# Two-layer encoder trunk, one core: the last token tile's norm and the routing around it

## Chip, core and metric

The kernel runs on one core of one Trainium2 chip. The metric is the device time of one execution in microseconds (us), lower is better. The kernel before takes 1039.52 us, the median of three runs between 1038.59 and 1041.96 us.

## The reference, cut to what matters

Each of two layers mixes 512 tokens of width 1024 and then sends every token to two of sixteen small experts. The change lies between the two parts:

```
x    = _layernorm(DEEPNORM_ALPHA * x + mix, ln1_g[l], ln1_b[l])
glog = einsum('bsd,dg->bsg', x, wg) + bg         # 4 group logits
gp, gi = top_k(softmax(glog), 1)                 # best group
elog = einsum('bsd,gde->bsge', x, we) + be       # 4 expert logits in each group
ep, ei = top_k(softmax(elog of group gi), 2)     # best two experts
h    = silu(x @ w_gate[e]) * (x @ w_up[e]) * combine
out  = h @ w_down[e]
```

The kernel has no top_k. It counts ranks by comparisons, and so gets for every token and expert a place in that expert's block of 96 rows.

## The kernel before, in words

The 512 tokens are four tiles of 128 (t0 to t3). Within a layer, after the mixer, the string `WSEQ` gives the order in which the steps of the four tiles are traced; a planner at compile time then orders each engine's instructions by that order and by when it reckons their inputs to be ready. `tc.issue_after(ins)` puts what is traced in its block behind `ins` on that instruction's own engine, in order of issue only. `pin` keeps instructions behind the one traced before them on their engine.

The steps of one tile i are: `m`/`n`/`o` products with the output projection; `e` evacuation, four transposes (TensorE) and a copy (ScalarE, `cp`); `b` mean and variance; `r` the reciprocal root; `l` eight small products with the routers' weights and `c` the correction of the logits by mean and root; `g` and `f` the norm itself, `(x - mean) * gain` and `* root + bias`; `k` a store to `acc`. `f` ends with the store of the tile to `x1d` (L1804), from which the experts' rows are gathered. Of the norm's 1024 columns the first `PHS[i]` = 512 go over ScalarE and GpSimd (L1793, L1801), the rest over VectorE. `Kab` is `route(a, b)` for tiles a to b-1: `ranks` and comparisons on VectorE, down to the mark `al` (which experts a token has); a product of `al` with a strict triangle and with ones (TensorE); `key` (the place in the block); and the one-hots `ohf` and `ohs` of experts 0 and 1.

Expert 0's rows are not gathered. `Zi` (`xz`) multiplies tile i with `ohf`, sixteen products, and sums all four tiles in two PSUM banks; after Z3 they are split in a high and a low part. `H` is `ex[1].go()`: products that give the row numbers of expert 1 (`slx`), and on GpSimd's queue the indirect gather from `x1d` (L1447), which needs the stores of all four tiles. Behind it on GpSimd stands a memset (`mark`), and loads of weights traced after it wait for that (`held`).

Then come the weights of the tokens (softmax values, some thirty small VectorE instructions), and `all_experts`: 24 products with the first weights of expert 0 (`up`), transposes of expert 1's gathered rows (`x`), and then a fixed order per expert. SyncE issues the weights' loads in the planner's order, and so does it with the stores.

Of the kernel before, what the change touches and what calls it, by code (L numbers as in the profile page):

```python
# [2 lines left out]

# [6 lines left out]
F32 = mybir.dt.float32  # L10
F32R = mybir.dt.float32r
BF = mybir.dt.bfloat16
I32 = mybir.dt.int32
# [4 lines left out]
D = 1024  # L18
# [66 lines left out]
HK = 0  # L85
HE = 0
WSEQ = ('S0 S1 S2 A m0 e0 b0 r0 r0 r0 r0 g0 A m1 e1 b1 r1 r1 r1 r1 g1 l0 c0 f0 k0 A m2 l1 c1 K02 e2 b2 r2 r2 r2 r2 g2 f1 k1 '
        'A n3 l2 c2 K23 Z0 o3 e3 b3 r3 r3 g3 r3 r3 l3 c3 f2 k2 K34 Z1 Z2 f3 H Z3')
WPIN = ''
NU = 7  # L90
WOG = (0, 2)
PTV = range(8)
GSEQ = 'gzgzgzgzzz'
PHS = (512, 512, 512, 512)
SQ = (0, 1, 2, 3)
SQN = ((), (0, 1, 2, 3))
PHASE = None
# [114 lines left out]
def tile_trunk(ctx: ExitStack, tc: tile.TileContext, ins, out, dbg=None, depth=DEPTH):  # L212
# [191 lines left out]
    V.memset(t64, 0.0)  # L404


    def split(dst_h, dst_l, src, eng=V):
        r = A.activation(dst_h, src, AF.Copy)
        eng.tensor_sub(dst_l, src, dst_h.bitcast(F32))
        return r  # L410

    def pair(src=None):
# [145 lines left out]
    for l in range(depth):  # L558
# [678 lines left out]
        def mla_in():  # L1237
            for i in range(2):
                b, h, lo = pair()
                split(h[64:96], lo[64:96], kra[64:96])  # L1240
                V.tensor_copy(h[96:128], h[64:96].bitcast(F32))
                V.tensor_copy(lo[96:128], lo[64:96].bitcast(F32))
# [36 lines left out]
            mla.update(rots=rots, qn=qn, kn=kn, uk=uk[0], vt=vt)  # L1279
            router_sums()  # L1280
            yield

        def load_uq(g):
# [124 lines left out]
        class Expert:  # L1408
# [56 lines left out]
            def xz(self, i, z):  # L1465
# [1 line left out]
                if i == 0:  # L1467
                    self.px = [P4.get(4 * BLK) for _ in range(2)]
                for k in range(KD):
                    T.matmul(self.px[k // 4][:, (k % 4) * BLK:(k % 4 + 1) * BLK], z[:, k * 128:(k + 1) * 128],  # L1470
                             self.ohf[:, i], start=i == 0 and k % 4 == 0, stop=i == NT - 1, skip_group_check=True)
                if i == NT - 1:
                    self.gth, self.gtl = Q.get(1024, full=True), Q.get(1024, full=True)
                    for q in range(2):
                        w = slice(q * 4 * BLK, (q + 1) * 4 * BLK)
                        split(self.gth[:, w], self.gtl[:, w], self.px[q].ap)
                    free(self.px)

            def weights(self, wts):

# [239 lines left out]
        prk = []  # L1720

        def route(a, b):

# [8 lines left out]
            V.tensor_tensor(al[:, a:b].rearrange("p i (g e) -> p i g e", g=4), oa[:, a:b], bc(oh1[:, a:b, 0]), op=OP.mult)  # L1732
            if not prk:
                prk.append(P5.get(NT * E))
            p = prk[0]
# [8 lines left out]
                T.matmul(v[:, i + 1:b], onesb, al[:, i, None, :].to_broadcast([128, b - 1 - i, E]),  # L1744
                         start=False, stop=False, skip_group_check=True)
            if a:
                T.matmul(p[:, a * E:b * E], strict, al[:, a:b].rearrange("p i e -> p (i e)"), start=False, stop=True,
                         skip_group_check=True)
            r = V.scalar_tensor_tensor(key[:, a:b], v[:, a:b], 1.0, al[:, a:b], op0=OP.add, op1=OP.mult)
            for e in range(2):  # L1750
                ex[e].hot(key[:, :, e], a, b)
# [2 lines left out]
        class Tile_:  # L1754
# [42 lines left out]
            def f(self):  # L1797
                z, n = self.z, self.ph
                if n:
                    self.cp = A.activation(z[:, 0:n], z[:, 0:n], AF.Identity, scale=self.rs)  # L1800
                    G.tensor_add(z[:, 0:n], z[:, 0:n], ln1[1][:, 0:n])  # L1801
                if n < D:
                    V.scalar_tensor_tensor(z[:, n:], z[:, n:], self.rs, ln1[1][:, n:D], op0=OP.mult, op1=OP.add)
                self.st = nc.sync.dma_start(x1d[self.s, :], z.ap)  # L1804

            def keep(self):
# [10 lines left out]
        for c in WSEQ.split():  # L1817
            if c[0] == "Z":
                i = int(c[1])
                ex[0].xz(i, tiles[i].z)  # L1820
                if i < NT - 1:
                    tiles[i].z.free()
                continue
# [12 lines left out]
            if c[0] == "S":  # L1836
# [2 lines left out]
                pin[0] = False  # L1839
                continue  # L1840
            t = tiles[int(c[1])]
            pin[0] = WPIN
            {"m": t.mm, "n": lambda: t.mm(range(PROG, 3)), "o": lambda: t.mm((3,)), "e": t.evac, "b": t.bn, "r": t.r, "l": t.logits, "c": t.lgs, "g": t.g, "f": t.f, "k": t.keep}[c[0]]()
            pin[0] = False
# [19 lines left out]
        ahead(RES3)  # L1864


        lv = lg.rearrange("p i (g e) -> p i g e", g=5)
        m1, m2 = small([128, NT, 5], tag="m1"), small([128, NT, 4], tag="m2")
        V.tensor_reduce(m1, lv, axis=AX.X, op=OP.max)
        ge = small([128, NT, 4], tag="ge")  # L1870
        V.tensor_tensor(ge, lv[:, :, 0], bc(m1[:, :, 0]), op=OP.subtract)
        A.activation(ge, ge, AF.Exp)
        gs = small([128, NT], tag="gs")
        V.tensor_reduce(gs, ge, axis=AX.X, op=OP.add)
        el2 = small([128, NT, 4, 4], tag="el2")
        V.scalar_tensor_tensor(el2, oh1[:, :, 1:5], NEG, lv[:, :, 1:5], op0=OP.mult, op1=OP.add)
        V.tensor_reduce(m2, el2, axis=AX.X, op=OP.max)
        V.tensor_sub(m2, m2, m1[:, :, 1:5])
        V.tensor_mul(m2, m2, oh1[:, :, 0])
        md = small([128, NT], tag="md")  # L1880
        V.tensor_reduce(md, m2, axis=AX.X, op=OP.add)
        A.activation(md, md, AF.Exp)
        wgt = small([128, 2, NT], tag="wgt")
        V.scalar_tensor_tensor(wgt[:, 0], md, 1.0, gs, op0=OP.add, op1=OP.mult)
        V.tensor_scalar(wgt[:, 0], wgt[:, 0], ALPHA, None, op0=OP.mult)
        V.reciprocal(wgt[:, 0], wgt[:, 0])
        V.tensor_mul(wgt[:, 1], wgt[:, 0], md)

        wt, wu = small([128, NT, E], tag="wt"), small([128, NT, 4, 4], tag="wu")
        wv = wt.rearrange("p i (g e) -> p i g e", g=4)  # L1890
        V.tensor_tensor(wu, oa, oh1[:, :, 1:5], op=OP.subtract)
        for o, c in ((wu, 1), (wv, 0)):
            V.tensor_tensor(o, wu if c else oh1[:, :, 1:5], wgt[:, c, :, None, None].to_broadcast([128, NT, 4, 4]), op=OP.mult)
        V.tensor_add(wv, wv, wu)
        V.tensor_tensor(wv, wv, ogx, op=OP.mult)
        for c in range(3):
            V.tensor_copy(tokw[:, :, :, c], wt)
            if c < 2:
                V.tensor_sub(wt, wt, tokw[:, :, :, c])

        pcn = P5.get(E)
        for i in range(NT):
            T.matmul(pcn.ap, onesb, al[:, i], start=(i == 0), stop=(i == NT - 1))
        more = small([128, 3, E], tag="more")
        nb, inc, off = more[:, 0], more[:, 1], more[:, 2]
        V.tensor_scalar(nb, pcn.ap, float(BLK), None, op0=OP.is_gt)
        for c in range(2 * BLK, S, BLK):
            V.scalar_tensor_tensor(nb, pcn.ap, float(c), nb, op0=OP.is_gt, op1=OP.add)
        pcn.free()
        V.tensor_tensor_scan(inc, nb, nb, 0.0, op0=OP.add, op1=OP.bypass)  # L1910
        V.tensor_sub(off, inc, nb)
        nblk = small([1, 1], I32, tag="nblk")
        V.tensor_copy(nblk, inc[0:1, E - 1:E])
        tap("lg%d" % l, lg.rearrange("p i c -> p (i c)"))
        tap("key%d" % l, key.rearrange("p i c -> p (i c)"))

        ph("moe")

        def all_experts():


            fw, fr, fr2 = (None, None), None, None
            for e in range(2):
                ex[e].weights(tokw[:, :, e, :])
            for q in range(4):
                ex[0].up(q)
            if E > 1:
# [303 lines left out]
```

## Time and profile before

| | us |
|---|---|
| median of three runs | 1039.52 |
| profiled execution, its own time | 1042.05 |
| span of the profiled execution | 1040.3 |

The span is the time from the first to the last instruction; the rest of the profiled execution's time lies around it. Its mean granted TensorE clock is 0.984 of full speed. Routing of layer 0 lies at about 320 to 349 us of the span, that of layer 1 at about 832 to 861 us. A timeline row gives the start, the busy time, the engine, the line, the operation and in brackets the engine's idle time before it with what ended it; a row may stand for several instructions (x16), whose times lie within it.

### The profile page before, as it was taken

To read this page: it belongs to the slowest core of one execution; us is meant where nothing else is said; L and a number is where in the kernel's file an instruction comes from. 1 tells how busy PE (TensorE), PEld (TensorE's weight loads), DVE (VectorE), ACT (ScalarE), POOL (GpSimd) and SP (SyncE) were. 2 spreads that over 40 slices of the span, in tenths; PEclk is the share of its full clock that TensorE was granted. 3 is DMA by queue.
4 is the path that set the end of the run, shared out by engine and by line. 5 is a ranking of instruction groups with operands and counts; after the bars stand their busy time and mean duration, and the time that the engine had idled before them with its cause. 6 is when DMAs were issued, how large, how long until landed. Compare 5 with 4: busy or idle time off the path is not lost. (4 is left out here: it accounts for less than half of the span.)

```text
span 1040.3 us, 15380 instructions
## 1 busy us (share of the span) xinstructions
PE 984.0 (95%) x5326; PEld 735.5 (71%) x5326; DVE 814.4 (78%) x1808; ACT 636.2 (61%) x1176; POOL 192.4 (18%) x176
## 2 busy tenths in 40 slices
PE   6999999999998999999899999999999989999995
PEld 6976697666687666766598767885757876666663
DVE  7996556878639799999778956578795498999986
ACT  5565625576424588889546556465673246888874
POOL 1000001242003133232000000022420122333332
PEclk9999989999999899999899999999999989999998
DMA  8201100015855889998541101001358387999944
GB/s 313 71 21 65 67 1 1 25 55 185 282 184 212 286 273 342 340 328 275 190 163 57 55 31 61 1 1 41 115 166 311 138 281 260 331 340 328 317 118 161
DMA packets 51793, 176.74 MB, mean 170 GB/s; under 512 B 8169, under 2 KB 8681, under 8 KB 51712
## 3 DMA queue, kind: packets, MB, share of 16 engines
q1 hardware_dynamic: 45216, 160.42, 43.3%
q0 software_dynamic: 6496, 15.31, 6.1%
q8 instruction: 42, 0.69, 0.3%
q14 instruction: 39, 0.32, 0.1%
HBM read 159.61 MB, written 23.59 MB: 176 GB/s over the span
## 5 line engine op out<-in xcount | busy, mean ns | idle before, releaser
L229 PE MATMUL b<-xt,s 128*128 128x512 f32 (+3 forms) x1484 | 327.4, 368 | 12.5 <-ACT s L229 8.5
L229 PE MATMUL b<-s,s 128*128 128x512 f32 (+8 forms) x1312 | 323.4, 404 | 4.7 <-ACT s L229 2.9
L229 PEld LDWEIGHTS b<-xt,s 128*128 128x128 f32 (+2 forms) x1484 | 234.8, 184 | 79.4 <-issue 12.8
L229 DVE TENSOR_TENSOR s<-s,s 128x1024 fp32r<-128x1024 f32 (+8 forms) x252 | 226.5, 924 | 53.1 <-ACT s L229 45.6
L229 ACT ACTIVATE s<-s 128x1024 fp32r<-128x1024 f32 (+4 forms) x221 | 192.3, 904 | 89.7 <-PE b L229 32.6
L229 PEld LDWEIGHTS b<-s,s 128*128 128x128 f32 (+3 forms) x1312 | 183.4, 171 | 85.9 <-ACT s L229 18.6
L229 ACT ACTIVATE s<-b 128x512 f32<-128x512 f32 (+8 forms) x274 | 132.2, 500 | 179.3 <-PE b L229 174.1
L229 PE MATMUL b<-s,xt 128*128 128x256 f32 (+2 forms) x944 | 204.6, 357 | 0.3 <-DVE s L229 0.3
L229 PEld LDWEIGHTS b<-s,xt 128*128 128x128 f32 (+1 forms) x944 | 147.9, 187 | 33.9 <-issue 6.9
L229 DVE TENSOR_TENSOR xt<-s,xt 128x1024 fp32r<-128x1024 f32 (+1 forms) x106 | 125.9, 1194 | 14.8 <-ACT xt L229 14.6
L229 ACT ACTIVATE xt<-s 128x1024 fp32r<-128x1024 f32 (+1 forms) x107 | 110.6, 1043 | 27.7 <-PE b L229 17.0
L229 PE MATMUL b<-ident,s 128*128 128x128 f32 (+3 forms) x736 | 106.0, 268 | 12.6 <-DMA s<-x1d,slx 6.2
L229 PEld LDWEIGHTS b<-ident,s 128*128 128x128 f32 (+3 forms) x736 | 80.6, 150 | 44.5 <-POOL s L1339 10.3
L1599 POOL DMA_INDIRECT acc<-s,slx x28 | 58.6, 2092 | 168.3 <-ACT s L229 128.5
L229 DVE TENSOR_TENSOR s<-b,s 128x192 fp32r<-128x192 f32 (+3 forms) x108 | 57.9, 549 | 12.6 <-PE b L229 10.1
L1339 POOL TENSOR_SCALAR s<-s,sums 128x512 f32<-128x512 f32 x48 | 37.3, 780 | 150.5 <-DVE sums L229 121.7
L229 ACT ACTIVATE s<-b,mx 128x512 f32<-128x512 f32 x64 | 44.0, 693 | 19.0 <-DVE mx L229 12.7
L1447 POOL DMA_INDIRECT s<-x1d,slx x30 | 40.5, 1349 | 55.3 <-PE b L229 16.1
L229 DVE TENSOR_REDUCE mx<-b 128x1 f32<-128x512 f32 x64 | 43.5, 687 | 8.7 <-PE b L229 7.9
L229 PE MATMUL b<-xt 128*96 128x512 f32 x160 | 47.1, 400 | 1.4 <-DVE xt L229 1.4
L229 ACT ACTIVATE s<-b,slw 96x512 f32<-96x512 f32 (+1 forms) x60 | 39.2, 684 | 6.4 <-PE b L229 4.3
L229 ACT ACTIVATE s<-s,sb 128x128 f32<-128x128 f32 x64 | 25.6, 413 | 20.4 <-DVE s L229 20.0
(249 smaller groups left out, 869.2 us busy)
## 6 DMA issues: line engine op xcount, KB each, us to landing
s<-in_w_gu_dram SPq DMA_DIRECT2D x128, 512.0 KB, 9.3
s<-in_expert_w_down_dram SPq DMA_DIRECT2D x64, 512.0 KB, 9.7
s<-in_w_inp_dram SPq DMA_DIRECT2D x36, 512.0 KB, 5.0
s<-in_w_outp_dram SPq DMA_DIRECT2D x16, 512.0 KB, 4.8
x1d<-s SPq DMA_DIRECT2D x8, 512.0 KB, 2.9
acc<-s SPq DMA_DIRECT2D x8, 512.0 KB, 4.3
s<-acc SPq DMA_DIRECT2D x8, 512.0 KB, 7.0
s<-in_x_t_dram SPq DMA_DIRECT2D x4, 512.0 KB, 5.4
```

What stands on the lines that cost most here:

```text
L229: r = f(*a, **kw)
L1339: (V if hd in NORMV else G).tensor_scalar(P.ap, P.ap, sums, 0.0, op0=OP.mult, op1=OP.add)
L1447: self.ga = G.indirect_dma_start(out=self.xg[:BLK], out_offset=None, in_=x1d[0:128 * n, :], in_offset=bass.IndirectOffsetOnAxis(ap=ix[:BLK ...
L1599: G.indirect_dma_start(out=acc[:, :], out_offset=bass.IndirectOffsetOnAxis(ap=self.ix[:BLK, 0:1], axis=0), in_=yt[:BLK], in_offset=None, b ...
```

## The change

The last tile's norm goes whole over VectorE: `PHS[3]` is 0. Its `g` is one instruction of 1024 columns, queued behind the `al` of tile t2; its `f` is two of 512, queued behind the `key` of tile t3. Since ScalarE has no part in `f` any more, `tiles[3].cp`, behind which ScalarE's work of the experts is queued, is the copy in `e`. `g3` and `K34` have other places in `WSEQ`. Before the strict product of t3 stand four bf16 products of 512 columns that nobody reads (`warm`), behind Z2, and four more behind it, ahead of Z3. The VectorE part of `router_sums` (of the following layer's routers) is queued behind an instruction of its own mixer part, the tokens' weights behind `key` of t3, and in `all_experts` their sums and expert 2's rows behind the low part of expert 1's first weight split; `ex[1].split(1)` is traced later.

```diff
-        'A n3 l2 c2 K23 Z0 o3 e3 b3 r3 r3 g3 r3 r3 l3 c3 f2 k2 K34 Z1 Z2 f3 H Z3')
+        'A n3 l2 c2 K23 Z0 o3 e3 b3 g3 r3 r3 r3 r3 l3 c3 f2 k2 Z1 Z2 K34 f3 H Z3')
-PHS = (512, 512, 512, 512)
+PHS = (512, 512, 512, 0)
+WARM = (4, 4)
...
-        eng.tensor_sub(dst_l, src, dst_h.bitcast(F32))
+        low[0] = eng.tensor_sub(dst_l, src, dst_h.bitcast(F32))
...
-            router_sums()
+            with tc.issue_after(rr.ins):
+                router_sums()
...
+        def warm(n, ins):
+            r = ins
+            if n:
+                p = P5.get()
+                with tc.issue_after(ins.ins):
+                    for _ in range(n):
+                        r = nc.tensor.matmul(p.v("p (a c) -> p a c", a=4), identb, onesb[:, None, :].to_broadcast([128, 4, 128]),
+                                             start=True, stop=True)
+                p.free()
+            return r
...
-                T.matmul(p[:, a * E:b * E], strict, al[:, a:b].rearrange("p i e -> p (i e)"), start=False, stop=True,
-                         skip_group_check=True)
+                last = b == NT
+                r = warm(WARM[0], zl[-1]) if last else None
+                with tc.issue_after(r.ins) if last else nullcontext():
+                    r = T.matmul(p[:, a * E:b * E], strict, al[:, a:b].rearrange("p i e -> p (i e)"), start=False, stop=True,
+                                 skip_group_check=True)
+                if last:
+                    zl.append(warm(WARM[1], r))
...
-                if n < D:
-                    V.scalar_tensor_tensor(z[:, n:], z[:, n:], self.rs, ln1[1][:, n:D], op0=OP.mult, op1=OP.add)
+                for a, b in ((n, D),) if n else ((0, 512), (512, D)):
+                    V.scalar_tensor_tensor(z[:, a:b], z[:, a:b], self.rs, ln1[1][:, a:b], op0=OP.mult, op1=OP.add)
                 self.st = nc.sync.dma_start(x1d[self.s, :], z.ap)
...
-                ex[0].xz(i, tiles[i].z)
+                with tc.issue_after(zl[-1].ins) if i == NT - 1 else nullcontext():
+                    zl.append(ex[0].xz(i, tiles[i].z))
...
+            if c in ("g3", "f3"):
+                with tc.issue_after(alv[-1].ins if c == "g3" else kins.ins):
+                    t.g() if c[0] == "g" else t.f()
+                continue
...
+        with tc.issue_after(kins.ins):
+            inc, off, nblk = expert_weights()
...
-            for e in range(2):
-                ex[e].weights(tokw[:, :, e, :])
             for q in range(4):
                 ex[0].up(q)
-            if E > 1:
-                ex[1].x()
-                ex[1].split(0)
-                ex[1].split(1)
-            for e in range(2, RA):
-                ex[e].rows(key[:, :, e])
-                ex[e].weights(tokw[:, :, e, :])
+            ex[1].x()
+            ex[1].split(0)
+            with tc.issue_after(low[0].ins):
+                for e in range(2):
+                    ex[e].weights(tokw[:, :, e, :])
+                for e in range(2, RA):
+                    ex[e].rows(key[:, :, e])
+                    ex[e].weights(tokw[:, :, e, :])
+            ex[1].split(1)
```

`expert_weights` holds the thirty small instructions in their old order; its body is not changed.

## Rows read from the trace of the kernel before

**Rows 1.** The page, part 1: busy time per engine

```profile
PE 984.0 (95%) x5326; PEld 735.5 (71%) x5326; DVE 814.4 (78%) x1808; ACT 636.2 (61%) x1176; POOL 192.4 (18%) x176
```

**Rows 2.** Stretches of layer 1: busy us per engine, granted clock, DMA share

```profile
846.87:849.50 2.63, 0.20 (x2) 0.12 (x2) 2.49 (x18) 2.00 (x4) 0.00 (x0) 0.92 0.72 231
849.50:853.40 3.90, 3.89 (x21) 3.90 (x21) 2.59 (x12) 1.95 (x4) 1.47 (x2) 0.50 0.96 325
```

**Rows 3.** Timeline, TensorE, layer 1: start us, us, operation, idle before

```profile
844.87 2.00 PE L229 MATMUL b<-ohf,s 128*128 128x96 f32 x16 [0.17 <-DVE ohf L229]
848.69 0.17 PE L229 MATMUL b<-al,strict 128*128 128x16 bf16 x1 [1.82 <-DVE al L229]
849.51 0.71 PE L229 MATMUL b<-ohf,s 128*128 128x96 f32 x2 [0.62 <-DVE ohf L229]
850.09 3.28 PE L229 MATMUL b<-ohf,s 128*128 128x96 f32 x14
853.47 2.72 PE L229 MATMUL b<-xt,s 128*96 128x512 f32 x6
856.04 2.94 PE L229 MATMUL b<-s,s 128*96 128x512 f32 x12
858.81 1.54 PE L229 MATMUL b<-xt,s 128*96 128x512 f32 x6
860.68 0.52 PE L229 MATMUL b<-ident,s 96*128 96x96 f32 x4 [0.33 <-DMA s<-x1d,slx]
```

**Rows 4.** Timeline, VectorE and GpSimd, layer 1, last tile's norm

```profile
844.81 0.23 DVE L229 SCALAR_TENSOR_TENSOR lg<-wsb,nmean,lg 128x20 f32<-128x20 f32 x1
844.96 0.75 DVE L229 SCALAR_TENSOR_TENSOR s<-s,nr,s 128x512 f32<-128x512 f32 x1
845.45 1.40 POOL L1801 TENSOR_TENSOR s<-s,s 128x512 f32<-128x512 f32 x1 [1.48 <-ACT s L229]
845.62 1.25 DVE L229 SCALAR_TENSOR_TENSOR lg<-lg,nr,wsb 128x20 f32<-128x20 f32 x1
```

**Rows 5.** Timeline, VectorE, layer 1: last tile's key and one-hots

```profile
848.90 0.17 DVE L229 SCALAR_TENSOR_TENSOR key<-b,al 128x16 f32<-128x16 f32 x1
849.28 0.25 DVE L229 TENSOR_TENSOR ohs<-iota,key 128x96 bf16<-128x96 bf16 x1
```

**Rows 6.** Timeline, SyncE's queue, VectorE, GpSimd, layer 1: store, loads, gather

```profile
846.87 0.32 SPq L1804 DMA_DIRECT2D x1d<-s  x1
847.30 1.20 SPq L276 DMA_DIRECT2D s<-in_expert_w_down_dram  x2
853.05 1.24 SPq L276 DMA_DIRECT2D s<-in_expert_w_down_dram  x2
850.46 0.15 DVE L229 SCALAR_TENSOR_TENSOR slx<-slr,b 96x1 int32<-96x1 f32 x1
851.55 1.36 POOL L1447 DMA_INDIRECT s<-x1d,slx  x1 [4.70 <-DMA s<-in_expert_w_down_dram]
```

**Rows 7.** DMA issues and a tile's answer: KB each, us to landing

```profile
x1d<-s SPq DMA_DIRECT2D x1, 512.0 KB, 2.9
s<-x1d,slx POOLq DMA_INDIRECT x1, 9.0
s<-x1d,slx POOLq DMA_INDIRECT x1, 6.2
DMA to landing us min/median/max: 2.6/8.3/10.1
```

**Rows 8.** Timelines, SyncE, GpSimd and TensorE, layer 0: store, gather, its reader

```profile
334.71 0.32 SPq L1804 DMA_DIRECT2D x1d<-s  x1
339.88 1.29 POOL L1447 DMA_INDIRECT s<-x1d,slx  x1 [5.19 <-DMA s<-in_expert_w_down_dram]
349.03 0.69 PE L229 MATMUL b<-ident,s 96*128 96x96 f32 x6 [0.51 <-DMA s<-x1d,slx]
```

**Rows 9.** Timeline, TensorE, layer 1, after the second expert's rows

```profile
864.32 2.58 PE L229 MATMUL b<-xt,s 128*96 128x512 f32 x10 [1.37 <-DVE s L229]
```

More of the change, by code (lines that the diff above doesn't have):

```diff
@@ L1 @@
 import math
-from contextlib import ExitStack
+from contextlib import ExitStack, nullcontext
 import concourse.bass as bass
@@ L404, in tile_trunk @@
     V.memset(t64, 0.0)
+    low = [None]
     def split(dst_h, dst_l, src, eng=V):
         r = A.activation(dst_h, src, AF.Copy)
[L409 removed]
+        low[0] = eng.tensor_sub(dst_l, src, dst_h.bitcast(F32))
         return r
@@ L1241, in mla_in @@
                 V.tensor_copy(h[96:128], h[64:96].bitcast(F32))
-                V.tensor_copy(lo[96:128], lo[64:96].bitcast(F32))
+                rr = V.tensor_copy(lo[96:128], lo[64:96].bitcast(F32))
                 kb.append((b, h, lo))
@@ L1469, in xz @@
                 for k in range(KD):
-                    T.matmul(self.px[k // 4][:, (k % 4) * BLK:(k % 4 + 1) * BLK], z[:, k * 128:(k + 1) * 128],
-                             self.ohf[:, i], start=i == 0 and k % 4 == 0, stop=i == NT - 1, skip_group_check=True)
+                    r = T.matmul(self.px[k // 4][:, (k % 4) * BLK:(k % 4 + 1) * BLK], z[:, k * 128:(k + 1) * 128],
+                                 self.ohf[:, i], start=i == 0 and k % 4 == 0, stop=i == NT - 1, skip_group_check=True)
                 if i == NT - 1:
@@ L1719, in tile_trunk @@
         key = small([128, NT, E], tag="key")
-        prk = []
+        prk, alv, zl = [], [], []
+        def warm(n, ins):
[7 more added lines that the diff above has]
+                p.free()
+            return r
         def route(a, b):
@@ L1731, in route @@
                             thr4[:, None, 0].to_broadcast([128, n * 5, 4]), op=OP.is_lt)
-            V.tensor_tensor(al[:, a:b].rearrange("p i (g e) -> p i g e", g=4), oa[:, a:b], bc(oh1[:, a:b, 0]), op=OP.mult)
+            alv.append(V.tensor_tensor(al[:, a:b].rearrange("p i (g e) -> p i g e", g=4), oa[:, a:b], bc(oh1[:, a:b, 0]),
+                                       op=OP.mult))
             if not prk:
@@ L1864, in tile_trunk @@
         ahead(RES3)
[L1867 to L1915, printed above, removed]
+        def expert_weights():
+            lv = lg.rearrange("p i (g e) -> p i g e", g=5)
+            m1, m2 = small([128, NT, 5], tag="m1"), small([128, NT, 4], tag="m2")
+            V.tensor_reduce(m1, lv, axis=AX.X, op=OP.max)
+            ge = small([128, NT, 4], tag="ge")
+            V.tensor_tensor(ge, lv[:, :, 0], bc(m1[:, :, 0]), op=OP.subtract)
+            A.activation(ge, ge, AF.Exp)
+            gs = small([128, NT], tag="gs")
+            V.tensor_reduce(gs, ge, axis=AX.X, op=OP.add)
+            el2 = small([128, NT, 4, 4], tag="el2")
+            V.scalar_tensor_tensor(el2, oh1[:, :, 1:5], NEG, lv[:, :, 1:5], op0=OP.mult, op1=OP.add)
+            V.tensor_reduce(m2, el2, axis=AX.X, op=OP.max)
+            V.tensor_sub(m2, m2, m1[:, :, 1:5])
+            V.tensor_mul(m2, m2, oh1[:, :, 0])
+            md = small([128, NT], tag="md")
+            V.tensor_reduce(md, m2, axis=AX.X, op=OP.add)
+            A.activation(md, md, AF.Exp)
+            wgt = small([128, 2, NT], tag="wgt")
+            V.scalar_tensor_tensor(wgt[:, 0], md, 1.0, gs, op0=OP.add, op1=OP.mult)
+            V.tensor_scalar(wgt[:, 0], wgt[:, 0], ALPHA, None, op0=OP.mult)
+            V.reciprocal(wgt[:, 0], wgt[:, 0])
+            V.tensor_mul(wgt[:, 1], wgt[:, 0], md)
+            wt, wu = small([128, NT, E], tag="wt"), small([128, NT, 4, 4], tag="wu")
+            wv = wt.rearrange("p i (g e) -> p i g e", g=4)
+            V.tensor_tensor(wu, oa, oh1[:, :, 1:5], op=OP.subtract)
+            for o, c in ((wu, 1), (wv, 0)):
+                V.tensor_tensor(o, wu if c else oh1[:, :, 1:5], wgt[:, c, :, None, None].to_broadcast([128, NT, 4, 4]), op=OP.mult)
+            V.tensor_add(wv, wv, wu)
+            V.tensor_tensor(wv, wv, ogx, op=OP.mult)
+            for c in range(3):
+                V.tensor_copy(tokw[:, :, :, c], wt)
+                if c < 2:
+                    V.tensor_sub(wt, wt, tokw[:, :, :, c])
+            pcn = P5.get(E)
+            for i in range(NT):
+                T.matmul(pcn.ap, onesb, al[:, i], start=(i == 0), stop=(i == NT - 1))
+            more = small([128, 3, E], tag="more")
+            nb, inc, off = more[:, 0], more[:, 1], more[:, 2]
+            V.tensor_scalar(nb, pcn.ap, float(BLK), None, op0=OP.is_gt)
+            for c in range(2 * BLK, S, BLK):
+                V.scalar_tensor_tensor(nb, pcn.ap, float(c), nb, op0=OP.is_gt, op1=OP.add)
+            pcn.free()
+            V.tensor_tensor_scan(inc, nb, nb, 0.0, op0=OP.add, op1=OP.bypass)
+            V.tensor_sub(off, inc, nb)
+            nblk = small([1, 1], I32, tag="nblk")
+            V.tensor_copy(nblk, inc[0:1, E - 1:E])
+            tap("lg%d" % l, lg.rearrange("p i c -> p (i c)"))
+            tap("key%d" % l, key.rearrange("p i c -> p (i c)"))
+            return inc, off, nblk
```

## The prediction

> **What bounds the kernel now.** I read the page's busy times first. TensorE is busy for 95% of the span [rows 1], so time is to be had only where it waits or runs at the lower clock. The stretches of the routing are such a place. In layer 1, TensorE works 0.20 of the 2.63 us from 846.87, and in the 3.90 us that follow the granted clock is 0.50, the 1.2 GHz level [rows 2]. The timeline of TensorE shows why: behind Z2, which ends at 846.87, it waits 1.82 us for `al` of t3; Z3 then takes from 849.51 to 853.37, and the first six `up` products take 2.72 us, 0.45 each, where the next twelve take 2.94, 0.245 each [rows 3]. VectorE's chain to `al` is held up by the norm: the second logit correction, 0.23 us in its sister instruction, takes 1.25 and ends at 846.87, when GpSimd's half of `f3` (845.45 to 846.85) has ended [rows 4]. So far the change aims at the right place.
>
> The reader is to see one row more. When the 24 `up` products end, at 860.35, TensorE waits for the gathered rows of expert 1 until 860.68 [rows 3]; in layer 0 the same wait is 0.51 us [rows 8]. So two paths end together: Z3 and `up` on one side, and on the other the gather, which starts at 851.55 [rows 6] and lands 9.0 us later, at 860.55 [rows 7]. Whoever shortens the first alone gains a third of a microsecond.
>
> **Part 1: up to the strict product.** GpSimd's two halves of t3's norm go, and with them the hold-up of 1.25 - 0.23 = 1.0 us [rows 4] and its like at `al` of t2. `al` of t3 then isn't what comes last. The strict product is now queued behind Z2 and four unread products. TensorE has no gap worth naming ahead of Z2's end but the 0.17 us of [rows 3], so Z2 ends at 846.7 at best. The trace has no bf16 product of 512 columns. It is bounded by the strict product, 0.17 us for 16 columns, and by the f32 ones of 512 columns, 0.245 at the full clock [rows 3]; I take the latter, as the columns are the same: 4 x 0.245 = 0.98 (0.68 to 0.98). Strict starts at 847.7 against 848.69, 1.0 us earlier. `g3`, now about twice the 0.75 us of [rows 4], lies on VectorE while TensorE does Z1 and the logits' products, and I cost it at nothing; if that cover is gone, it is late by under 1.5 us and the unread products cover 1.0 of it. The tokens' weights and `router_sums`, held behind `key` or moved to the mixer, take nothing from TensorE; they free some slots of 0.1 to 0.3 us ahead of an `al` that is no longer last: nothing.
>
> **Part 2: `f3`.** It moves from beside the chain to behind `key`. Before: its VectorE half at 844.96 and GpSimd's until 846.85 [rows 4]. After: `key` at 848.90 - 1.0 = 847.9; the one-hots stand ahead of it, so it starts 0.55 behind `key` (the last one-hot starts 0.38 behind it and holds the engine some 0.17 [rows 5]), at 848.45. Two halves at 0.75 [rows 4] end at 849.2 and 849.95. Z3's first eight products can start at 849.2. With four more unread products in the wait I take the clock as full: Z3 takes the 2.00 us of Z2 [rows 3] and ends at 851.2, not 853.37. The 24 `up` products take 24 x 0.245 = 5.9 against 6.9, and end at 857.1 instead of 860.35. This path gains 3.2 us a layer.
>
> **Part 3: the store and the gather.** The last store to `x1d` goes out when `f3` ends: at 846.87 before [rows 6], now at 849.95, 3.1 us later. It lands after 2.9 us [rows 7], or about 3.5 with loads beside it, at 852.85 to 853.45. Before, the store wasn't what the gather waited for: it had landed at 849.8, and the gather started 0.95 us behind the end of `slx`, at 850.6 [rows 6] (the profile names a load as the releaser, which the index fits better). `slx` comes earlier now, so the store decides. A start between 0.1 and 0.95 us behind the landing gives 852.95 to 854.4; I take 853.15, 1.6 us later than 851.55. Behind the store SyncE's queue has the loads that the planner puts there, and behind the gather GpSimd has the memset and thereby the held loads; none of them is needed before expert 3, so their delay costs nothing by itself. Layer 0 has the same rows 512 us earlier: store at 334.71, gather at 339.88 [rows 8].
>
> How long the gather takes hangs on the loads beside it. Those of layer 1 stand on SyncE's queue right behind the store [rows 6], and two more follow the memset behind the gather, at 853.05 [rows 6]. Over the whole trace gathers and stores land in 2.6 to 10.1 us; with the DMA engines full in both routings it was 9.0, and a later one of layer 1 took 6.2 [rows 7]. A load or two may now pass the later store, but the gather, the store, the copy of t3 to `acc` and the held loads still keep the engines full: I take 9.0, and 6.2 as the other end. It lands at 862.15, and TensorE goes on at 862.3 instead of 860.68: 1.6 us a layer lost.
>
> A rule of the skill speaks for less. The Trainium skill, DMA: Bandwidth & Descriptors (Queues, rings and completion order), says that each DMA engine takes turns, packet by packet, between the queues it has work for. A gather of 0.39 MB (96 rows of 4 KB) with half of 325 GB/s [rows 2] would then land some 2.4 us after GpSimd has issued it, not 7.6; [rows 7] do not show that, and by the rule the sum would be that of the third rival.
>
> **Part 4: behind the gather.** TensorE now idles from 857.1 to 862.3 but for small products. In [rows 2, 3] a wait of 1.8 us and a broken second were enough for the lower clock, so I expect it here: twelve `up` products of expert 1 at 0.45 instead of 0.245 cost 2.5 us. Against that stand the wait of 1.37 us for a split in [rows 9], which VectorE can do while TensorE waits for the gather, and the index and weight products that move into the wait, about 0.7. Net 0.4; as an order in which the planner may not put them, I set it between -2.0 (clock stays full) and +2.5, and take 0.
>
> **Sum.** 2 x (+1.6 + 0) = +3.2 us. The profiled execution takes 1042.05 us (span 1040.3, 1.75 around it), and so 1045.25 after; it lies 2.5 above the median of 1039.52, on which the same sum gives 1042.7.
>
> **Rivals.** First, faster: the gather isn't late, because loads that stood behind the store are issued ahead of it, in the slack before 849.95, and find the engines empty again. For it speaks that t3's store is ready 3 us later and SyncE has nothing else to do; against it that the store itself then shares with them. It decides once the gather lands within 7.0 us of its start (860.15). At 6.2 us it lands at 859.35, 1.2 earlier; with the 1.37 of [rows 9] saved, 2.6 a layer: 1034.3. The most it could give is the whole 3.2 and the 1.37: 1030.4.
>
> Second, balance: the gather lands within half a microsecond of before, the clock and the saved split cancel: 1039.5, within 1.5 us either way.
>
> Third, the gather gets an equal share of the DMA engines beside any load. It would land by 857 in both layers, TensorE would not wait, and with 3.2 a layer the time is 1033. The rule above says so; against it are the 9.0 us of [rows 7], so its chance is small.
>
> Fourth, worse: the lower clock stays through all products of expert 1 and the start of expert 2, adding 2.5 us a layer to the 1.6: 1047.7.
>
> Fifth, the unread products don't keep the clock, so that Z3 and `up` take as long as before. `up` would end at 860.2, before the gather still; the time is that of the forecast, since that path isn't last.
>
> **Chances.** Forecast with the fifth rival, 0.42, between 1040.5 and 1045: about 0.30 of it is more than 0.3% (3.1 us, what a measurement here tells from no change) slower, 0.12 within. Worse 0.08. Balance 0.20, all within. First rival 0.24 and third 0.06, all faster. So faster 0.30, same 0.32, slower 0.38. The forecast's own range is 1040.5 to 1045; the one that holds 8 in 10 leaves out the far end of the gains and of the fourth rival: 1034 to 1047.
>
> **What would show it.** Right: no hold-up in the second logit correction of t3; the strict product about 1 us earlier behind Z2; Z3 in about 2 us at the full clock; t3's store 3 us later than 846.87; the gather 1 to 2.5 us later and its reader the longest wait of TensorE in the stretch, above 3 us, with a granted clock of 0.5 behind it. Wrong: a gather that lands before 860 in layer 1, or a TensorE that finds other work in that wait. If `up` of expert 0 ends at 857 and the gather's wait is under 1 us, the forecast has failed at part 3.

## The result, and the profile after

The changed kernel takes 1047.13 us (median of eight runs, 1043.10 to 1048.23) against 1039.55 us before (eight runs beside it): a ratio of 1.0066, 95% interval 1.0045 to 1.0086. That is slower by two thirds of a per cent, clear of noise: 6.9 us by the ratio, 7.6 between the two medians. The forecast was 1042.7 and the wide range ended at 1047.0. By the ratio the time is 1046.4 on the forecast's 1039.52, near that end and near the fourth rival's 1047.7.

The profiled execution of after took 1043.10 us (span 1041.3), the fastest of its eight; the one of before, 1042.05, was slower than its median. The two traces alone would show 1.0 us of the loss, so I took a second profile (`again`, below) and compare by stretches. First TensorE in layer 1 of the first profile of after; the columns are those of [rows 3].

```profile
845.03 1.03 PE L1734 MATMUL b<-onesb,identb 128*128 128x512 bf16 x4
845.92 0.17 PE L230 MATMUL b<-al,strict 128*128 128x16 bf16 x1
...
848.41 1.11 PE L230 MATMUL b<-ohf,s 128*128 128x96 f32 x8
849.30 1.61 PE L230 MATMUL b<-xt,s 128*96 128x512 f32 x6
...
853.53 1.54 PE L230 MATMUL b<-xt,s 128*96 128x512 f32 x6
859.80 1.54 PE L230 MATMUL b<-ident,s 96*128 96x96 f32 x8 [4.73 <-DMA s<-x1d,slx]
861.94 0.40 PE L230 MATMUL b<-tokr,ohs 128*96 128x2 bf16 x4 [0.60 <-DVE s L230]
862.71 1.04 PE L230 MATMUL b<-tokw,ohs 128*96 128x3 bf16 x12 [0.36 <-DVE slr L230]
863.61 4.78 PE L230 MATMUL b<-xt,s 128*96 128x512 f32 x12
```

Against [rows 3]: the strict product no longer waits 1.82 us for `al`; Z3, which took 3.9 us, and the six `up` products, 2.72, run at the full clock. But the 0.33 us in front of expert 1's transposes have become 4.73. The stretches of the same trace (busy us of PE, PEld, DVE, ACT, POOL, then granted clock, DMA share, GB/s) show the lower clock of [rows 2] in another place:

```profile
850.00:855.00 5.00, 5.00 (x22) 3.23 (x20) 5.00 (x20) 3.27 (x6) 1.23 (x2) 1.00 0.96 332
855.00:859.80 4.80, 0.07 (x2) 0.01 (x1) 2.96 (x9) 1.32 (x2) 0.00 (x0) 0.73 0.92 289
859.80:864.00 4.20, 3.24 (x25) 3.05 (x26) 1.91 (x10) 0.98 (x2) 0.00 (x0) 0.50 0.44 176
864.00:868.20 4.20, 4.20 (x12) 2.66 (x11) 0.41 (x1) 0.00 (x0) 0.99 (x1) 0.58 0.22 61
868.20:872.00 3.80, 3.80 (x27) 2.96 (x26) 3.39 (x8) 3.16 (x6) 1.27 (x1) 1.00 0.50 152
```

VectorE's timeline answers to [rows 4, 5]: the second logit correction is back at 0.24 us, and `f3` stands behind `key`, one half ahead of the one-hots.

```profile
843.71 0.24 DVE L230 SCALAR_TENSOR_TENSOR lg<-lg,nr,wsb 128x20 f32<-128x20 f32 x1
846.14 0.17 DVE L230 SCALAR_TENSOR_TENSOR key<-b,al 128x16 f32<-128x16 f32 x1 [0.45 <-PE b L230]
846.23 0.74 DVE L230 SCALAR_TENSOR_TENSOR s<-s,nr,s 128x512 f32<-128x512 f32 x1
847.23 0.74 DVE L230 SCALAR_TENSOR_TENSOR s<-s,nr,s 128x512 f32<-128x512 f32 x1
```

SyncE's queue and the gather, and their times to landing (store, gather), answer to [rows 6, 7]. Two loads of w_down and one of w_gu now go ahead of t3's store; the store lands after 4.6 us, the gather after 6.2. In layer 0 these are 5.8 and 4.4. The gather starts 1.0 us after the store has landed (848.00 + 4.6 = 852.6, against 853.60), in layer 0 1.1 us.

```profile
843.06 2.50 SPq L277 DMA_DIRECT2D s<-in_expert_w_down_dram  x2
845.61 0.43 SPq L277 DMA_DIRECT2D s<-in_w_gu_dram  x1
848.00 0.33 SPq L1827 DMA_DIRECT2D x1d<-s  x1
853.60 1.12 POOL L1451 DMA_INDIRECT s<-x1d,slx  x1 [16.64 <-DVE wgt L230]
...
x1d<-s SPq DMA_DIRECT2D x1, 512.0 KB, 4.6
s<-x1d,slx POOLq DMA_INDIRECT x1, 6.2
```

The absolute times of the traces can't be laid over each other, as the mixers differ by single spells of the lower clock. So I count from t2's store to `x1d`, which lies ahead of the changed part (838.41 before, 836.99 after in layer 1), and end at the issue of the fourth gather, by when the experts run in their rhythm. Each number is a difference of two starts in the timelines of SyncE, GpSimd and TensorE, in us, layer 0 / layer 1. "Rows read" is the start of expert 1's transposes; "sum" is what the two layers' fourth gathers come later than before's, added up; "measured" is the measured ratio, less one, times 1039.5.

| | t3's store | gather of expert 1 | rows read | fourth gather | sum | measured |
|---|---|---|---|---|---|---|
| before | 8.46 / 8.46 | 13.63 / 13.14 | 22.78 / 22.27 | 40.04 / 39.55 | | |
| after, first profile | 10.74 / 11.01 | 17.64 / 16.61 | 22.09 / 22.81 | 40.78 / 42.47 | +3.7 | +6.9 |
| after, `again` | 10.73 / 11.02 | 16.20 / 16.71 | 23.30 / 23.48 | 42.24 / 43.22 | +5.9 | +6.0 |
| e1 no unread products | 10.56 / 10.82 | 16.53 / 16.46 | 23.42 / 23.91 | 42.42 / 44.31 | +7.1 | +5.5 |
| e2 rows not from x1d | 10.73 / 11.02 | 12.02 / 12.23 | 19.82 / 21.62 | 38.29 / 42.21 | +0.9 | +1.8 |
| e3 early f3 | 7.89 / 7.89 | 13.81 / 12.77 | 21.59 / 21.38 | 39.56 / 39.27 | -0.8 | +0.3 |
| e4 loads behind store | 10.73 / 10.73 | 14.78 / 15.08 | 24.61 / 24.50 | 44.16 / 44.24 | +8.8 | +9.6 |
| e5 holds alone | 8.45 / 8.46 | 13.20 / 13.15 | 23.56 / 23.71 | 43.06 / 42.99 | +6.5 | +5.3 |
| e6 norm alone | 10.88 / 10.73 | 17.77 / 17.63 | 22.46 / 21.88 | 41.46 / 42.57 | +4.4 | +4.9 |
| e8 wait filled | 10.73 / 11.02 | 17.22 / 17.57 | 23.12 / 23.96 | 42.17 / 42.90 | +5.5 | +2.6 |
| e9 early f3, filled | 7.90 / 8.16 | 13.57 / 15.32 | 21.13 / 22.66 | 38.97 / 42.36 | +1.7 | +3.7 |
| e11 early f3, no holds | 8.00 / 7.89 | 14.62 / 14.25 | 21.02 / 22.90 | 39.62 / 42.16 | +2.2 | +1.5 |
| e12 early f3, loads held | 7.89 / 7.89 | 14.19 / 12.70 | 19.25 / 19.39 | 39.36 / 38.03 | -2.2 | -2.8 |
| e13 order alone | 8.45 / 8.45 | 13.33 / 13.13 | 22.38 / 22.85 | 41.80 / 42.05 | +4.3 | +2.0 |

One profiled execution a kernel is little, and single sums are off by up to 3.2 us. But the sums follow the measured times roughly, from -2.2 (e12) to +8.8 (e4), so most of the loss lies between t2's store and the fourth gather of the two layers.

### The profile page after: what moved, and what is told of

Read it like the earlier page. It is cut to its first block, busy times and chain, and to the rows that moved or that the text cites. A ratio compares the mean times of both kernels' runs of the same rounds, so it can differ in the third digit from the quotient of the medians.

```text
span 1041.3 us, 15398 instructions
## 1 busy us (share of the span) xinstructions
PE 985.1 (95%) x5342; PEld 733.1 (70%) x5342; DVE 812.8 (78%) x1810; ACT 632.6 (61%) x1172; POOL 187.4 (18%) x172
## 5 line engine op out<-in xcount | busy, mean ns | idle before, releaser
L230 ACT ACTIVATE s<-s,sb 128x128 f32<-128x128 f32 x64 | 25.6, 413 | 19.4 <-DVE s L230 19.1
```

Source lines behind the costliest of these rows:

```text
L230: r = f(*a, **kw)
```

## The experiments

Theory: t3's store goes out late, so the gather is late, TensorE waits for its rows and runs at the lower clock behind that wait. Rivals: the unread products cost the time; the held weights and the order in front of the experts cost it.

**again.** The changed kernel unchanged.

> The changed kernel once more, for a second profile: the first one was of an execution some 4 us faster than the median of its runs. Theory (the clock behind the wait): the missing time stands in the experts behind the gather, as a longer wait or a lower clock that lasts longer: from the store of t2 to the third gather 31.5 to 34.5 us in layer 0 (31.0 in the first profile) and 32.7 to 35 in layer 1 (32.7). Rival: it stands in the mixers, where the first profile has a granted clock of 0.88 to 0.95 in one place only, and the two stretches stay within 0.5 us of the first profile's. Time 1045 to 1048.5 us.

1045.11 us, ratio 1.0058 (1.0035 to 1.0081). The sum of the stretches is +5.9 us, the measured loss 6.0. From t2's store to the third gather it took 33.1 and 33.4 us, as the theory had it, against 31.0 and 32.7 in the first profile. TensorE in layer 1, and its stretches:

```profile
860.98 1.54 PE L230 MATMUL b<-ident,s 96*128 96x96 f32 x8 [5.36 <-DMA s<-x1d,slx]
864.80 4.85 PE L230 MATMUL b<-xt,s 128*96 128x512 f32 x12
...
855.60:861.00 5.40, 0.04 (x2) 0.02 (x1) 2.88 (x9) 1.32 (x2) 0.00 (x0) 0.78 0.89 274
861.00:864.80 3.80, 2.83 (x25) 2.66 (x25) 1.63 (x8) 0.98 (x2) 0.00 (x0) 0.50 0.31 124
864.80:869.60 4.80, 4.80 (x17) 3.20 (x17) 0.69 (x4) 0.00 (x0) 0.99 (x1) 0.58 0.17 54
```

The wait ends 0.5 and 1.2 us later than before (23.30 - 22.78, 23.48 - 22.27), and from there to the fourth gather it takes 1.7 and 2.5 us longer: 1.7 us of the loss are the late rows, 4.1 what lies behind them, where the granted clock is 0.50. In the first profile the rows were not late at all, summed over the layers (22.09 and 22.81 against 22.78 and 22.27): its 3.7 us lie wholly behind them. TensorE's wait is long there because `up` ends earlier.

**e1_nowarm.**

```diff
-WARM = (4, 4)
+WARM = (0, 0)
```

> The changed kernel without its eight unread products. Main theory (the late store of t3 and the gather behind it cost the time): TensorE loses the full clock in the wait for the strict product and Z3 and `up` of expert 0 take up to 3 us longer, but they still end before the gathered rows of expert 1 come, so the time stays at that of the changed kernel, 1045.5 to 1048.5 us, and the wait for the rows shrinks from 4.3 and 4.7 us to 1.5 to 3. Rival (the unread products themselves cost the time): the time falls by 2 us or more, below 1045.

1045.1 us, ratio 1.0053 (1.0031 to 1.0075): no difference that can be told from the changed kernel's. The median lies at the edge between the two expectations, but the intervals overlap almost wholly. The reason that I gave holds in layer 0 alone. In layer 1 TensorE kept the clock without the unread products; in layer 0 it fell to 0.51 from 335.6 to 338.3 us, behind waits of 0.55 and 1.07 us. First layer 1, then `up` of expert 0 in layer 0:

```profile
846.93 0.17 PE L230 MATMUL b<-al,strict 128*128 128x16 bf16 x1 [0.54 <-DVE al L230]
848.19 0.46 PE L230 MATMUL b<-ohf,s 128*128 128x96 f32 x2 [1.07 <-DVE ohf L230]
850.30 1.62 PE L230 MATMUL b<-xt,s 128*96 128x512 f32 x6
862.08 1.54 PE L230 MATMUL b<-ident,s 96*128 96x96 f32 x8 [6.01 <-DMA s<-x1d,slx]
...
335.64 2.84 PE L230 MATMUL b<-xt,s 128*96 128x512 f32 x6
338.29 3.33 PE L230 MATMUL b<-s,s 128*96 128x512 f32 x12
```

In layer 1 the waits are only 0.54 and 1.07 us, and Z3 ends 12.1 us behind t2's store (850.30 - 838.17; after 849.30 - 836.99 = 12.3). In layer 0 `up` ends 1.4 us later behind t2's store than in the changed kernel, but the wait for the rows, still 4.21 us, hides that. So without the unread products the clock fell in one of the two layers, and the time shows no loss from it.

**e2_free.**

```diff
-in_=x1d[0:128 * n, :],
+in_=(x1d[0:128 * n, :] if self.e != 1 else dram(ins["x"], 0, [[D, 128 * n], [1, D]])),
```

> The changed kernel with expert 1 gathering its rows from the kernel's input x and not from the normalized tiles, so that its gather does not wait for t3's store (the rows of expert 1 are those of x, nothing else is left out). Main theory: the gather starts about 1 us behind slx, 3.5 to 4.5 us earlier in each layer, TensorE's wait for the rows falls from 4.3 and 4.7 us to under 1.5, and the time to 1037 to 1041 us. Rival (the moved weights of the tokens and the order of the experts' work cost the time): the wait goes, but other waits take its place and the time stays above 1044.

1041.38 us, ratio 1.0017 (0.9999 to 1.0035): 4 to 5 us are given back (0.41% and 0.49% of 1039.5, against the two measurements of the changed kernel), just short of what the theory expected. TensorE's wait fell to 2.04 and 3.54 us, not under 1.5. The gather goes out 4.4 us earlier in layer 1 (16.61 to 12.23), but lands only after 9.3 us, so its rows come 1.2 us earlier than in the first profile of after, 1.9 earlier than in `again`. GpSimd, TensorE, and the time to landing:

```profile
845.25 1.05 POOL L1451 DMA_INDIRECT s<-in_x_dram,slx  x1 [12.26 <-DVE slx L230]
854.64 1.54 PE L230 MATMUL b<-ident,s 96*128 96x96 f32 x8 [3.54 <-DMA s<-in_x_dram,slx]
858.95 5.20 PE L230 MATMUL b<-xt,s 128*96 128x512 f32 x12
...
s<-in_x_dram,slx POOLq DMA_INDIRECT x1, 9.3
```

So the store's landing is a real part of the loss, but not all: with a wait of 3.54 us the lower clock stays in layer 1. In layer 0, with a wait of 2.04 us, the transposes took 0.88 us.

**e3_early.**

```diff
-... b3 g3 r3 r3 r3 r3 l3 c3 f2 k2 Z1 Z2 K34 f3 H Z3')
+... b3 g3 r3 r3 r3 r3 f3 l3 c3 f2 k2 Z1 Z2 K34 H Z3')
-                with tc.issue_after(alv[-1].ins if c == "g3" else kins.ins):
+                with tc.issue_after(alv[-1].ins) if c == "g3" else nullcontext():
```

> The changed kernel with f3 ahead of the second logit correction of t3 instead of behind key: still whole on VectorE, in the chain. Main theory: the chain to key is 1.4 us later, the store goes out about 3.9 us earlier and lands before slx is ready, the gather starts some 3 us earlier in each layer, `up` of expert 0 ends about 1.3 us later, TensorE's wait for the rows falls to 0.5 to 2 us, and the time to 1039 to 1043 us. Rival (the held order behind key costs, not the store): the chain is longer by 1.4 us and the time rises by 2 to 3 us, to 1049 or more.

1038.78 us, ratio 1.0003 (0.9982 to 1.0024). No loss that can be told from zero is left, slightly better than the main theory expected, with every other part of the change still there. Layer 1, SyncE, GpSimd, TensorE:

```profile
841.02 0.33 SPq L1827 DMA_DIRECT2D x1d<-s  x1
845.90 1.05 POOL L1451 DMA_INDIRECT s<-x1d,slx  x1 [12.80 <-DVE m L230]
854.51 0.88 PE L230 MATMUL b<-ident,s 96*128 96x96 f32 x8 [1.99 <-DMA s<-x1d,slx]
857.03 4.31 PE L230 MATMUL b<-xt,s 128*96 128x512 f32 x12
```

Behind t2's store, t3's store goes out 3 us earlier than in the changed kernel, the rows come 0.5 to 2.1 us earlier, and the transposes stay at the full clock (0.88 us; the twelve `up` products behind them don't, 4.31).

**e4_after_store.**

```diff
-            m.load(n)
+            with tc.issue_after(tiles[NT - 1].st.ins) if _ > 2 else nullcontext():
+                m.load(n)
```

> The changed kernel with the last four loads of the routing (the ones that pass t3's store in the trace: two of w_down, two of w_gu) held on SyncE behind that store. If those loads beside the store are what makes its landing 4.6 and 5.8 us instead of 2.9 and 3.2: it lands in about 3 us, the gather starts 1.5 to 2.5 us earlier, though it then shares with these loads and may take 7 to 9 us instead of 6.1 and 4.4; time 1043 to 1048 us, nearly even. Rival (the loads belong ahead of the store, the store's lateness alone counts): landing unchanged and time unchanged within 1 us, or slower because the gather takes 9 us: 1048 to 1051.

The edit does not hold the loads that I named. In its trace four loads of w_gu stand right behind the store (849.14 us in layer 1), the two of w_down still go ahead of it (843.83), and the two of w_gu that the changed kernel issues long before (832.36) no longer do. So the gather has more loads beside it than the store's place alone would give.

1049.15 us, ratio 1.0092 (1.0070 to 1.0115): slower still, and in the rival's range through the gather's 9 us, though the store did land sooner, as the theory said. Times to landing in layer 1 (store, gather) and the rows' reader:

```profile
x1d<-s SPq DMA_DIRECT2D x1, 512.0 KB, 3.4
s<-x1d,slx POOLq DMA_INDIRECT x1, 9.4
...
862.54 1.54 PE L230 MATMUL b<-ident,s 96*128 96x96 f32 x8 [6.70 <-DMA s<-x1d,slx]
```

The store lands 1.2 us sooner, and the gather behind the four loads takes 3.2 us more, 9.4 us (9.8 in layer 0). The Trainium skill, DMA: Bandwidth & Descriptors (Queues, rings and completion order), has each DMA engine take turns between the queues; the equal share that the prediction worked out from this, some 2.4 us behind the issue, is not what these 9.4 us show.

**e5_holds.** The change without its part on the norm (`PHS`, `g3`, `f3`, `WSEQ` and TensorE's order as before, no unread products).

```diff
-PHS = (512, 512, 512, 0)
-WARM = (4, 4)
+PHS = (512, 512, 512, 512)
+WARM = (0, 0)
...
-            if c in ("g3", "f3"):
+            if c in ():
```

> The other half of the change alone: router_sums in the mixer, the tokens' weights behind key and the new order in front of the experts, but t3's norm, the order of the steps and TensorE's waits as before (no unread products). Main theory: the store goes out as early as before, the gather isn't late, and the time is 1037.5 to 1041.5 us, that of the kernel before within 2 us. Rival (the held weights and the order of the experts' work cost the time): 1044 us or more.

1045.5 us, ratio 1.0051 (1.0030 to 1.0073). My theory missed this, and the rival holds: the held weights and the order in front of the experts cost 5.3 us alone, with a store and a gather as early as before. TensorE in layer 1:

```profile
857.44 4.36 PE L230 MATMUL b<-s,s 128*96 128x512 f32 x12
...
870.74 1.53 PE L230 MATMUL b<-ident,s 96*128 96x96 f32 x8 [1.96 <-DMA s<-x1d,slx]
```

Two things differ from before. The twelve middle `up` products of expert 0 take 4.36 us (4.22 in layer 0), where [rows 3] have 2.94: the lower clock behind Z3 lasts longer. And the second gather goes out 27.3 to 29.2 us behind t2's store (25.1 to 25.6 before), so that TensorE waits again, for expert 2 (0.83 us in layer 0, 1.96 in layer 1; 0.21 and 0.53 before).

**e6_norm.** The other half: no hold on router_sums or the weights, the work in front of the experts as before.

```diff
-            with tc.issue_after(rr.ins):
-                router_sums()
+            router_sums()
...
-        with tc.issue_after(kins.ins):
-            inc, off, nblk = expert_weights()
+        inc, off, nblk = expert_weights()
...
+            for e in range(2):
+                ex[e].weights(tokw[:, :, e, :])
             for q in range(4):
                 ex[0].up(q)
...
```

> The norm's part of the change alone: t3's norm whole on VectorE with f3 behind key, the moved steps and the eight unread products, but router_sums, the tokens' weights and the work in front of the experts as before. The other part alone had cost 5.3 us, against what I expected, and the whole change 5 to 7.7. If the two parts cost through one and the same place (TensorE waits for expert 1's rows or their split and runs at the lower clock behind it) and don't add up: 1043 to 1046 us, with the wait for the rows at 4 us or more and the tokens' weights done ahead of it. Rival (only the order in front of the experts costs, the late store nothing): 1038.5 to 1041. Second rival (they add up: 7 less 5): 1041 to 1042.5.

1043.68 us, ratio 1.0047 (1.0031 to 1.0063): the halves cost 4.9 and 5.3 us, the whole 6.0 to 6.9. They don't add up, as the first expectation had it: TensorE waited 4.54 and 4.08 us for expert 1's rows. Both halves end in a wait of TensorE for gathered rows; that the one wait hides part of the other is my reading, not shown by itself.

**e8_keep.** The function `warm` once more, behind the last `up` product `r` of expert 0.

```diff
...
             for q in range(4):
-                ex[0].up(q)
-            ex[1].x()
+                r = ex[0].up(q)
+            with tc.issue_after(warm(16, r).ins):
+                ex[1].x()
```

> The changed kernel with 16 more unread products (16 x 0.245 = 3.9 us) between `up` of expert 0 and the transposes of expert 1, in the wait of 4.3 and 4.7 us. If the lower clock behind the wait is the larger part of the loss: the rows come when they came, but the eight transposes take 0.85 us instead of 1.54 and the twelve first `up` products of expert 1 some 3 us instead of 4.8, so 2 to 3 us a layer are given back: 1041 to 1043.5 us. Rival (the wait itself is the loss, the clock next to nothing): 1045.5 to 1049.

1042.8 us, ratio 1.0025 (1.0007 to 1.0042): the time is where the clock theory put it, but the trace does not bear out why.

```profile
852.82 3.63 PE L1735 MATMUL b<-onesb,identb 128*128 128x512 bf16 x16
858.85 0.92 PE L230 MATMUL b<-ident,s 96*128 96x96 f32 x8 [2.41 <-DMA s<-x1d,slx]
861.47 5.25 PE L230 MATMUL b<-xt,s 128*96 128x512 f32 x12
...
858.80:863.00 4.20, 3.68 (x28) 3.21 (x29) 1.89 (x8) 0.87 (x2) 0.35 (x1) 0.59 0.34 138
```

The transposes keep the clock, but it falls behind them, and the twelve `up` products take 5.25 us, no less than after. By the table the profiled execution still loses 5.5 us in the stretches. Some 3.4 to 4.3 us of the median are given back, against the two measurements of the changed kernel; where that gain lies stays open.

**e9_both.** e3 with `WARM = (8, 4)` and `warm(8, r)` in the wait.

> The kernel with the early f3 (1038.8 us), with eight unread products instead of four ahead of the strict product (it waited 1.0 us for `al`) and eight more in the wait of 2.0 to 2.2 us for expert 1's rows. If the clock behind these shorter waits still costs something (the twelve `up` products of expert 1 took 4.31 us in layer 1, at the full clock 2.94): 0.5 to 1.5 us a layer are given back, 1035.5 to 1038 us, faster than the kernel before. Rival: the waits are short enough already and the unread products only delay what comes in time: 1038.5 to 1041.

1043.84 us, ratio 1.0036 (1.0016 to 1.0056): neither expectation; with more unread products e3 was slower by some 3 us, just clear of noise. In its profile the gather of layer 1 goes out later (15.32 us behind t2's store, 12.77 in e3); whether the unread products do that is not shown.

**e11_early_norm.** e3 with the three edits of e6.

> The early f3 (1038.8 us with the holds) without the other part of the change: router_sums, the tokens' weights and the work in front of the experts as before. If the order in front of the experts costs by itself (expert 2's rows start 2 to 3 us later because their index products are held behind the split of expert 1): the gather of expert 2 goes out 1 us or more earlier than with the holds and the time is 1034 to 1037.5 us, faster than the kernel before. Rival (the holds cost only behind before's norm, as expert 1's split came right behind a slow Z3 there): 1038 to 1041.

1042.24 us, ratio 1.0014 (0.9996 to 1.0031): not the gain I expected. Expert 2's gather goes out earlier than in e3 in layer 0 (23.61 against 25.12 us behind t2's store), but not in layer 1 (25.65 against 25.07). With the store early no cost of the holds shows; the two intervals overlap, so that they gain is not shown either.

**e12_loads.** e3, with two loads of w_gu held behind the memset that follows the gather.

```diff
-        for _ in range(NU):
+        for _ in range(5):
...
         held[0] = (None, kins, ...)[HOLD]
...
+        for _ in range(NU - 5):
+            m, n = todo.pop(0)
+            m.load(n)
```

> The early f3 with two of the loads of w_gu, that stood on SyncE between t3's store and its copy to acc, held behind the mark, so behind the issue of expert 1's gather. If the gather is late because its rows queue up behind loads: store and gather land sooner, TensorE's wait of 2.0 to 2.2 us for the rows falls under 1 us, and the time to 1035 to 1037.5 us. Rival (the loads then come beside the gather, which takes as long): within 1.5 us of 1038.8.

1037.16 us, ratio 0.9973 (0.9959 to 0.9987): faster than the kernel before, by 2.8 us, and than the changed one by some 9. SyncE, GpSimd, TensorE, layer 1:

```profile
853.51 1.05 POOL L1451 DMA_INDIRECT s<-x1d,slx  x1 [12.72 <-DVE m L230]
854.71 0.80 SPq L277 DMA_DIRECT2D s<-in_w_gu_dram  x2
860.20 0.88 PE L230 MATMUL b<-ident,s 96*128 96x96 f32 x8
862.17 0.48 PE L230 MATMUL b<-tokw,ohs 128*96 128x3 bf16 x8 [1.10 <-DVE tokw L230]
863.20 4.57 PE L230 MATMUL b<-xt,s 128*96 128x512 f32 x12
```

The gather takes 6.6 us instead of 8.6 (4.6 instead of 7.7 in layer 0), and the transposes follow `up` without a wait. The store does not land sooner (3.9 and 5.4 us, 4.0 and 5.0 in e3). What is left is 1.1 us for the tokens' weights and a lower clock behind it.

**e13_order.** The kernel before with the changed front of `all_experts` (held behind `low[0]`) alone.

> The kernel before with one edit alone: the tokens' weights of the first experts and the rows of expert 2 held behind the first split of expert 1 (router_sums, the start of the weights, the norm and the rest of the routing as before). If this order is what made the held half of the change cost 5.3 us: the gather of expert 2 goes out 2 to 3.5 us later behind t2's store than before (25.1 to 25.6 us there), TensorE waits for its rows or for the split with nothing to fill the wait, and the time is 1043 to 1046 us. Rival (the weights' start behind key, or router_sums in the mixer, cost it): 1038 to 1041.5 us.

1041.08 us, ratio 1.0019 (0.9992 to 1.0046): unclear, with the median on the rival's side. The second gather is late in both layers (27.98 and 26.53 us; 2 to 3.5 us later was expected, 2.3 and 1.4 it is), but by the medians that is worth 2 us of the 5.3, and the interval overlaps that of e5. Which hold makes the rest, and why the lower clock lasted longer in e5, stays open; in e13 the same twelve products took 3.90 us in layer 0 and 2.94 in layer 1.

## Where the prediction was right, and where wrong

The direction and the path were as forecast: the gather of expert 1 goes out late, TensorE's longest wait is for its rows (4.3 to 5.5 us), and the clock behind it is 0.50. The size was not: 6.0 and 6.9 us measured, 3.2 forecast. The term that was mis-sized is Part 4, put at nothing, some 2 us a layer measured. The measured time lies at the very end of the wide range, which is no merit of the sum, and "slower" had a chance of only 0.38.

**Part 1** was right: no hold-up, the strict product 0.9 us behind the end of Z2 (845.92 against 845.03), 1.0 forecast as the unread products' price. That it takes these to keep the clock was borne out in layer 0 of e1 and not in its layer 1.

**Part 2** was right in its gain: in layer 1 [rows 3] have `up` ending 21.9 us behind t2's store (860.35 - 838.41), after it is 18.1 (855.07 - 836.99), 3.9 us against 3.2 forecast. And as [rows 3] said, a third of a microsecond of it was to be had.

**Part 3** had the right wait, and a total that is near by luck, as its terms are off both ways. Behind t2's store, t3's store was 2.3 to 2.6 us later, not 3.1, as the planner put half of `f3` ahead of the one-hots. The store landed in 4.6 to 5.8 us, not 2.9 to 3.5. As I read it, that is because loads had passed it (the first rival's loads, which hurt where that rival had them help); in e4, with the last of these loads (of w_gu) behind the store instead of ahead of it, it landed in 3.0 and 3.4 us. The gather started 1.0 to 1.1 us behind the landing, just past the far end of the 0.1 to 0.95 that the prediction had, where it took 0.3. So the gather went out 2.6 to 4.0 us later, not 1.6. Its rows came 4.4 to 7.1 us behind its issue, not 9.0 (as I read it, because those loads had mostly landed by then). Together the rows were 0.9 us a layer late in `again`, not 1.6, and not late in the first profile. Store and gather together took 11.4 to 12.6 us from issue to reader, against 13.8 to 14.3 before.

**Part 4** is the step that failed. "Net 0.4; ... I set it between -2.0 (clock stays full) and +2.5, and take 0." The lower clock behind the wait came as forecast; from the rows to the fourth gather it took 1.7 and 2.5 us longer in `again` (1.4 and 2.4 in the first profile), up to the upper bound. In layer 1 the clock's own price was even higher, 2.9 us: from the transposes to the end of the twelve `up` products TensorE took 8.7 us in `again`, 1.0 of it waits (860.98 to 869.65), and 6.2 before, 1.4 of it a wait (860.68 to 866.90). Little came back against it: the wait of 1.37 us [rows 9] went, but 0.60 and 0.36 us for the split and the index products took its place. The index and weight products did not move into the wait: they stand behind the transposes (861.94, 862.71), and the first of them waits for VectorE's split of the rows. Z3 and `up` had run at that clock before too [rows 2], but there the gather hid it; now it lies behind the gather, where nothing does. The Trainium skill, TensorE: Matmul & The Clock Gate (HAM oscillation), tells of the same: a wait for a DMA leaves the work behind it at the lower clock. The trace agrees, with 0.50 behind waits of 4.7 and 5.4 us.

**The weights and the order** that I cost at nothing cost 5.3 us where before's norm is kept (e5), against no cost that shows where the norm is early (e11 and e3). In the whole change they add about 1 to 2 (6.0 and 6.9 against e6's 4.9), which noise could make.

**The rivals.** The fourth, at 1047.7 with a chance of 0.08, came nearest in time, and in part in mechanism: its price is that of Part 4's upper bound, but the lower clock ended after twelve of expert 1's 24 `up` products. The first rival's condition, a gather that lands within 7.0 us of its start, was met (6.2 and 4.4 us), and the gain did not come, since the start was later than that rival had it. The third fell with 9.3 us (e2) and 9.4 us (e4) for a gather beside loads. The fifth's condition did not arise in the changed kernel. With Part 4 at `again`'s 2.1 us a layer and Part 3 at its 0.9, the sum is +6.0, and 1045.5 on the median.

## What to carry to other kernels

When two paths end together, shortening one alone gains next to nothing, and the wait that it opens has a price of its own: here 4.1 of 5.9 us lie behind it. Before moving a norm behind a chain, follow its store to the reader, with the loads that will pass it in the queue; where the store went out early and two loads were held behind the gather, the same change was faster than before. Price the clock behind a new wait at its full cost, unless a row shows work that hides it.

## What the runs showed of the hardware

Single executions have spells of the lower clock with TensorE busy throughout. These are stretches in the middle of the mixers: of layer 0 and of layer 1 in the one profile of before, and of layer 1 in the first profile of after.

```profile
130.00:140.00 10.00, 10.00 (x71) 9.90 (x70) 6.98 (x32) 1.46 (x4) 0.00 (x0) 0.78 0.00 0
...
650.00:660.00 10.00, 10.00 (x85) 9.65 (x84) 6.93 (x35) 2.93 (x10) 0.00 (x0) 1.00 0.00 1
...
645.00:655.00 10.00, 10.00 (x72) 9.60 (x71) 7.05 (x37) 2.19 (x8) 0.00 (x0) 0.83 0.00 1
```

A mean of 0.78 over 10 us is 4.4 us at the lower level, some 2.2 us of work lost; 0.83 is 1.7. In all three stretches TensorE had just done 24 products of a single column (`ones,s`: 132.73 and 135.23, 649.54 and 652.04 in before, 645.10 and 647.72 in after). The clock fell behind them in one layer of each of these two profiles and not in the other. What decides that is not shown; it is one reason why single profiles differ by some 2 us.

The same goes for short waits: in e1 the waits of 0.54 and 1.07 us in layer 1 left the clock full, those of 0.55 and 1.07 in layer 0 did not.

And 3.6 us of unread products in a wait of 6.0 kept the clock for the eight transposes only: from 858.8 to 863.0 it was 0.59 (e8).
